# Instance norm on one core: five engine programs without the block around them

## The chip, the cores and the metric

One core of a Trainium2 chip. The metric is the device time of one execution in microseconds (us), as the median of several. The span in a profile is a little shorter, because it runs from the first to the last instruction. Ratios are the mean time of one kernel's runs over the mean of the other's in the same rounds, so not quite the ratio of the medians that are quoted beside them.

## The reference

```python
x: (8, 64, 32, 64, 64) float32          # 512 instances of 131072 values
mean = np.mean(x, axis=(2, 3, 4), keepdims=True)
var  = np.var(x, axis=(2, 3, 4), keepdims=True)
return ((x - mean) / np.sqrt(var + eps)).astype(np.float32)
```

256 MiB come in and 256 MiB go out: 268.44 MB each way.

## The kernel before

A tile is 128 partitions x 8192 values, 4 MiB, with 8 instances of 16 partitions each. Six tiles ("slots") are in flight. SyncE issues the loads. VectorE and ScalarE each sum one half. TensorE averages over partitions. ScalarE squares, takes the root, scales one half and issues the store, while VectorE scales the other half. GpSimd only builds two small matrices at the start. Everything is ordered by hand-placed semaphores (counters that engines count up and wait on), one set per slot. Each engine runs a hardware loop of 10 rounds of six tiles and then five straight-line pieces (three tiles and two half tiles).

The parts that the change touches:

```python
    ctx.enter_context(tc.tile_critical(name="norm"))
    # ... buffers, semaphores, on_vector, on_scalar, on_tensor, over_tiles (cut) ...

    block = ctx.enter_context(nc.Block())

    @block.sync
    def _(eng):
        for s in range(SLOTS):
            eng.dma_start(out=slots[s][:], in_=x_t[s]).then_inc(landed[s], 16)
        # ... loop over the other rounds, each load waiting for its slot's store (cut) ...

    @block.gpsimd
    def _(eng):
        # ... the two matrices and eps, counting up `ready` (cut) ...

    @block.vector
    def _(eng):
        over_tiles(eng, on_vector)

    @block.tensor
    def _(eng):
        eng.wait_ge(ready, READY)
        over_tiles(eng, on_tensor)

    @block.scalar
    def _(eng):
        eng.wait_ge(ready, READY)
        over_tiles(eng, on_scalar, with_target=True)
        for s in range(SLOTS):
            uses = ROUNDS + sum(1 for r in rest if r[3] == s)
            eng.wait_ge(stored[s], 16 * uses)          # all stores have landed
        for s in range(SLOTS, LANES):
            eng.wait_ge(stored[s], 16)
```

An all-engine barrier is a point that no engine passes before all five have come. Three things end this program, one inside the other: the block's exit (line `_compat.py:109` in the profile), the critical section's exit (line 42), and the end of the whole program (the line of the context around the kernel: 271 before, 260 after).

Of the kernel before, what the change touches and what calls it, by code (L numbers as in the profile page):

```python
# [9 lines left out]
def kernel(  # L10
# [6 lines left out]
    nc = tc.nc  # L17
# [11 lines left out]
    SLOTS = 6  # L29
    FULL = P * COLS // n_elem  # L30
    n_tiles = n_inst // FULL
    ROUNDS = (n_tiles - 1) // SLOTS
    LANES = SLOTS + 2
# [10 lines left out]
    def sbuf(name, shape, dtype=fp32):  # L44
        return ctx.enter_context(nc.sbuf_tensor(name, shape, dtype))
# [5 lines left out]
    avg = {n: sbuf(f"avg{n}", [P, P]) for n in (FULL, FULL // 2)}  # L51
# [6 lines left out]
    def semaphores(name, n):  # L58
        return [ctx.enter_context(nc.semaphore(f"{name}{i}")) for i in range(n)]

    ready = semaphores("ready", 1)[0]
# [10 lines left out]
    stored = semaphores("stored", LANES)  # L72
# [61 lines left out]
    def on_tensor(eng, t, lane, n, c1, c2, c16):  # L134
# [17 lines left out]
    rest = [  # L152
        (x_t[k], out_t[k], slots[k % SLOTS][:], k % SLOTS, k // SLOTS + 1, FULL)
        for k in range(ROUNDS * SLOTS, n_tiles - 1)
    ]
# [6 lines left out]
    def over_tiles(eng, step, with_target=False):  # L162
        counts = [
            ctx.enter_context(eng.register(f"{step.__name__}_c{m}")) for m in (1, 2, 16)
        ]
        for c, m in zip(counts, (1, 2, 16)):
            eng.reg_mov(c, m)
        with eng.Fori(0, ROUNDS) as it:
            for s in range(SLOTS):
                more = (out_t[it * SLOTS + s],) if with_target else ()  # L170
                step(eng, slots[s][:], s, FULL, *counts, *more)
            for c, m in zip(counts, (1, 2, 16)):
                eng.reg_add(c, c, m)
        for _, dst, t, lane, c, n in rest:
            more = (dst,) if with_target else ()
            step(eng, t, lane, n, c, 2 * c, 16 * c, *more)

    block = ctx.enter_context(nc.Block())

    @block.sync  # L180
    def _(eng):
        for s in range(SLOTS):
            eng.dma_start(out=slots[s][:], in_=x_t[s]).then_inc(landed[s], 16)
        c16 = ctx.enter_context(eng.register("load_c16"))
        eng.reg_mov(c16, 16)
        with eng.Fori(1, ROUNDS) as it:
            for s in range(SLOTS):
                eng.dma_start(out=slots[s][:], in_=x_t[it * SLOTS + s])._wait_ge(
                    stored[s], c16
                ).then_inc(landed[s], 16)  # L190
            eng.reg_add(c16, c16, 16)
        for src, _, t, lane, c, n in rest:
            behind = lane if lane < SLOTS else last
            uses = c - 1 if lane < SLOTS else ROUNDS
            eng.dma_start(out=t, in_=src)._wait_ge(stored[behind], 16 * uses).then_inc(
                landed[lane], 16
            )

    @block.gpsimd
    def _(eng):  # L200
        count = 0
        for n, m in avg.items():
            split = P // n

            eng.memset(m[:], 1.0 / n_elem).then_inc(ready, 1)  # L205
            count += 1
            for sign in (-1, 1):
                eng.affine_select(  # L208
                    out=m[:],
                    in_=m[:],  # L210
                    pattern=[[sign * split, n], [0, split]],
                    compare_op=Alu.is_ge,
                    fill=0.0,
                    base=0 if sign < 0 else split - 1,
                    channel_multiplier=-sign,
                )._wait_ge(ready, count).then_inc(ready, 1)
                count += 1
        eng.memset(eps_t[:], eps_f).then_inc(ready, 1)

    READY = 3 * len(avg) + 1  # L220

    @block.vector
    def _(eng):
        over_tiles(eng, on_vector)

    @block.tensor
    def _(eng):
        eng.wait_ge(ready, READY)
        over_tiles(eng, on_tensor)

    @block.scalar
    def _(eng):
        eng.wait_ge(ready, READY)
        over_tiles(eng, on_scalar, with_target=True)

        for s in range(SLOTS):
            uses = ROUNDS + sum(1 for r in rest if r[3] == s)
            eng.wait_ge(stored[s], 16 * uses)
        for s in range(SLOTS, LANES):
            eng.wait_ge(stored[s], 16)  # L240


# [33 lines left out]
```

## Time and profile before

| | before |
|---|---|
| time, median of 3 (range) | 1248.47 us (1248.38 to 1248.61) |
| span of the profile | 1246.9 us |
| busiest compute engine | ScalarE, 79% |
| transfers, 120 to 1130 us | share 1.00, 433 GB/s |
| from ScalarE's last wait records to the end | 1245.4 to 1246.9 us |

The lines behind this table stand in the prediction. Read them in this order. First the engine shares: none is full. Then the transfers: they are full. Then the two ends, because a block can only act at its entry and at its exit. A line of an engine's name with q (SPq, ACTq) is a record of that engine's sequencer: a branch, a drain, a semaphore record. The last two numbers ahead of the semicolon are the start of the first and of the last such record. The views round these starts to 0.1 us. Where this text gives hundredths, they are the time stamps that the trace keeps.

### The profile page before, as it was taken

The numbers are of one execution on the slowest core, as the hardware profiler recorded it, in microseconds if no ns is written. First come the engines' busy times: TensorE is split into PE (matmuls) and PEld (weight loads), VectorE is DVE, ScalarE is ACT, GpSimd is POOL, SyncE is SP. The second block draws the span as 40 slices with busy tenths as digits, with TensorE's granted clock in tenths as the row PEclk, the third lists the DMA queues.
The fourth block names the chain that finished last, engine by engine and source line by source line (L and its number), as shares of the span: only waits on it lengthen the run. The fifth ranks groups of instructions, "written<-read, shape, count | busy, mean of one in ns | idle before, by whom it ended". The sixth has DMA issues, their size and how long they took to land.

```text
span 1246.9 us, 1819 instructions
## 1 busy us (share of the span) xinstructions
PE 76.4 (6%) x260; PEld 65.2 (5%) x260; DVE 467.9 (38%) x325; ACT 986.1 (79%) x410; POOL 1.9 (0%) x11
## 2 busy tenths in 40 slices
PE   0000000000000000000000000000000000000000
PEld 0000000000000000000000000000000000000000
DVE  2344334433334334343343433433334333343331
ACT  5888888887787878778777878787787878778774
POOL 0000000000000000000000000000000000000000
DMA  9999999999999999999999999999999999999998
GB/s 403 422 435 427 433 436 435 428 433 436 435 428 433 437 434 429 432 436 435 431 430 436 436 434 425 437 436 435 427 434 436 435 428 433 436 435 428 433 432 376
DMA packets 18723, 536.90 MB, mean 431 GB/s; under 512 B 2081, under 2 KB 2081, under 8 KB 2081
## 3 DMA queue, kind: packets, MB, share of 16 engines
q1 hardware_dynamic: 9360, 268.44, 50.0%
q10 hardware_dynamic: 9360, 268.44, 49.9%
q14 instruction: 3, 0.02, 0.0%
HBM read 268.44 MB, written 268.44 MB: 431 GB/s over the span
## 4 chain that ended last, share of the span: by engine, by line
ACT 48%; DVE 29%; another core or an unknown queue 13%; PE 6%; issue 1%; DMA 1%; ACTq 0%; DVEq 0%; SPq 0%
ACT unused L113 37%; DVE small L79 18%; DVE slot L95 8%; ACT slot L123 4%; ACT unused L107 4%; PE psum L136 3%; PE psum L143 3%; ACT small L120 1%; ACT L120 1%; DMA slot<-in_x_dram 1%; DVE small L89 1%; DVE small L82 1%; DVE small L92 1%; ACTq L130 0%
## 5 line engine op out<-in xcount | busy, mean ns | idle before, releaser
L113 ACT ACTIVATE unused<-slot,small 128x8192 uint8<-128x8192 f32 (+1 forms) x65 | 456.1, 7017 | 90.1 <-DVE small L82 90.1
L79 DVE TENSOR_REDUCE small<-slot 128x1 f32<-128x4096 f32 (+1 forms) x65 | 282.9, 4353 | 164.4 <-DMA slot<-in_x_dram 164.4
L107 ACT ACTIVATE unused<-slot 128x4096 uint8<-128x4096 f32 (+1 forms) x65 | 231.7, 3564 | 82.1 <-DMA slot<-in_x_dram 77.0
L123 ACT ACTIVATE slot<-slot,small 128x4096 f32<-128x4096 f32 (+1 forms) x65 | 243.7, 3749 | 27.6 <-DVE small L92 27.6
L89 DVE RECIPROCAL small<-small 128x1 f32<-128x1 f32 x65 | 10.6, 164 | 533.8 <-ACT small L120 533.8
L95 DVE TENSOR_SCALAR slot<-slot,small 128x4096 f32<-128x4096 f32 (+1 forms) x65 | 154.7, 2379 | 2.4
L136 PE MATMUL psum<-small,avg 128*128 128x2 f32 x130 | 38.2, 363 | 674.1 <-DVE small L79 548.7
L136 PEld LDWEIGHTS psum<-small,avg 128*128 128x128 f32 x130 | 32.6, 311 | 679.6 <-DVE small L79 553.0
L143 PE MATMUL psum<-small,avg 128*128 128x1 f32 x130 | 38.2, 363 | 480.6 <-ACT unused L113 480.6
L143 PEld LDWEIGHTS psum<-small,avg 128*128 128x128 f32 x130 | 32.7, 312 | 486.2 <-ACT unused L113 486.2
L120 ACT ACTIVATE small<-psum,eps_t 128x1 f32<-128x1 f32 x65 | 17.0, 261 | 37.4 <-PE psum L143 37.3
L82 DVE TENSOR_REDUCE small<-psum 128x1 f32<-128x2 f32 x65 | 10.3, 159 | 62.5 <-PE psum L136 62.5
L107 ACT ACT_TABLE_LOAD x10 | 12.8, 1283 | 10.4 <-ACT slot L123 7.1
L120 ACT ACT_TABLE_LOAD x10 | 12.8, 1283 | 0.2
L107 ACT ACTIVATION_READ_ACCUMULATOR unused<-slot 128x1 f32 x65 | 12.1, 186 | 0.0
L113 ACT ACTIVATION_READ_ACCUMULATOR unused<-slot,small 128x1 f32 x65 | 12.1, 186 | 0.0
L92 DVE TENSOR_TENSOR small<-small 128x1 f32<-128x1 f32 x65 | 10.3, 159 | 2.2
L208 POOL TENSOR_SCALAR_AFFINE_SELECT avg<-avg 128x128 f32<-128x128 f32 x4 | 1.3, 324 | 0.3
L205 POOL MEMSET avg<- 128x128 f32 x2 | 0.4, 204 | 0.5 <-SPq L42 0.5
L257 POOL MEMSET const-bfloat16-1.0<- 128x1 bf16 x1 | 0.1, 101 | 0.0
L257 POOL MEMSET const-uint8-127<- 128x1 uint8 x1 | 0.1, 101 | 0.0
L257 POOL MEMSET const-float32-0.0<- 128x1 f32 x1 | 0.1, 98 | 0.3 <-issue 0.3
(2 smaller groups left out, 0.2 us busy)
## 6 DMA issues: line engine op xcount, KB each, us to landing
slot<-in_x_dram SPq DMA_DIRECT2D x63, 4096.0 KB, 52.8
out_dram<-slot ACTq DMA_DIRECT2D x63, 4096.0 KB, 45.3
slot<-in_x_dram SPq DMA_DIRECT2D x2, 2048.0 KB, 55.6
out_dram<-slot ACTq DMA_DIRECT2D x2, 2048.0 KB, 14.7
```

Of the source, the lines that this page charges most:

```text
L79: eng.reduce_sum(out=a[:, 0:1], in_=t[:, :w], axis=mybir.AxisListType.X)._wait_ge(landed[lane], c16).then_inc(summed[lane], 1)
L82: eng.tensor_reduce(out=a[:, 2:3], in_=psum[lane][:, 0:2], axis=mybir.AxisListType.X, op=Alu.add, negate=True,)._wait_ge(meaned[lane], c1) ...
L89: eng.reciprocal(out=a[:, 5:6], in_=a[:, 4:5])._wait_ge(rooted[lane], c1).then_inc(scaled[lane], 1)
L92: eng.tensor_mul(out=a[:, 6:7], in0=a[:, 2:3], in1=a[:, 5:6])._wait_ge(scaled[lane], c1).then_inc(shifted[lane], 1)
L95: eng.tensor_scalar(out=t[:, w:], in0=t[:, w:], scalar1=a[:, 5:6], scalar2=a[:, 6:7], op0=Alu.mult, op1=Alu.add,)._wait_ge(shifted[lane], ...
L107: eng.activation(out=unused[:, w : 2 * w], in_=t[:, w:], func=Act.Identity, accum_out=a[:, 1:2],)._wait_ge(landed[lane], c16).then_inc(sum ...
L113: eng.activation(out=unused[:, : 2 * w], in_=t, func=Act.Square, bias=a[:, 2:3], accum_out=a[:, 3:4],)._wait_ge(centred[lane], c1).then_in ...
L120: eng.activation(out=a[:, 4:5], in_=psum[lane][:, 2:3], func=Act.Sqrt, bias=eps_t[:, 0:1])._wait_ge(varied[lane], c1).then_inc(rooted[lane ...
L123: eng.activation(out=t[:, :w], in_=t[:, :w], func=Act.Identity, scale=a[:, 5:6], bias=a[:, 6:7],)._wait_ge(shifted[lane], c1).then_inc(don ...
L136: eng.matmul(out=psum[lane][:, 0:2], lhsT=avg[n][:], rhs=a[:, 0:2], start=True, stop=True,)._wait_ge(summed[lane], c2).then_inc(meaned[lan ...
L143: eng.matmul(out=psum[lane][:, 2:3], lhsT=avg[n][:], rhs=a[:, 3:4], start=True, stop=True,)._wait_ge(squared[lane], c1).then_inc(varied[la ...
L208: eng.affine_select(out=m[:], in_=m[:], pattern=[[sign * split, n], [0, split]], compare_op=Alu.is_ge, fill=0.0, base=0 if sign < 0 else s ...
```

## The change

Its intent is to shed what a block adds around five engine programs that have their own semaphores anyway. The programs become plain calls, one behind another, inside the critical section.

```diff
-    block = ctx.enter_context(nc.Block())
-
-    @block.sync
-    def _(eng):
+    def load_all(eng):
         ...
-    @block.gpsimd
-    def _(eng):
+    def set_up(eng):
         ...
-    READY = 3 * len(avg) + 1
-    @block.vector
-    def _(eng):
-        over_tiles(eng, on_vector)
-    ... tensor, scalar likewise (cut) ...
+        return count + 1
+
+    load_all(nc.sync)
+    set_by = set_up(nc.gpsimd)
+    over_tiles(nc.vector, on_vector)
+    nc.tensor.wait_ge(ready, set_by)
+    over_tiles(nc.tensor, on_tensor)
+    nc.scalar.wait_ge(ready, set_by)
+    over_tiles(nc.scalar, on_scalar, with_target=True)
+    ... the waits for the stores, on nc.scalar (cut) ...
```

## The prediction

> **What bounds the kernel now.** I read the page from the top, then the transfer queue's waits, a table of stretches, one tile in the timeline, and last the two ends of the program, because the change touches only the ends.
>
> The page first:
>
> ```profile
> span 1246.9 us, 1819 instructions
> PE 76.4 (6%) x260; PEld 65.2 (5%) x260; DVE 467.9 (38%) x325; ACT 986.1 (79%) x410; POOL 1.9 (0%) x11
> ...
> DMA  9999999999999999999999999999999999999998
> ...
> HBM read 268.44 MB, written 268.44 MB: 431 GB/s over the span
> ```
>
> No compute engine is full: ScalarE at 79% comes closest. The transfer engines are at nine tenths or more in 39 of 40 slices. The stretches of the run tell the same with more digits (columns: stretch, its length, busy time of PE, PEld, DVE, ACT, POOL, then clock, transfer share, GB/s):
>
> ```profile
> 1.20:13.50 12.30, 0.00 (x0) 0.00 (x0) 0.00 (x0) 1.28 (x1) 1.51 (x7) 1.00 0.94 384
> ...
> 120.00:1130.00 1010.00, 62.27 (x212) 53.20 (x212) 381.70 (x262) 812.97 (x335) 0.00 (x0) 1.00 1.00 433
> ...
> 1234.00:1246.90 12.90, 0.00 (x0) 0.00 (x0) 0.00 (x0) 0.00 (x0) 0.00 (x0) 1.00 0.70 300
> ```
>
> From 120 to 1130 us the transfer share is 1.00 at 433 GB/s. One tile is 4 MiB in and 4 MiB out, 8.39 MB; 8.39 MB / 433 GB/s = 19.4 us. In the timeline the square pass of two successive late tiles starts at 1160.79 and 1180.21 us, 19.42 us apart, so tiles come at the pace of the transfers. ScalarE has 812.97 / 1010 = 80% in that stretch and sits idle for the rest. The load queue confirms who waits:
>
> ```profile
> SPq L188 <- DMA out_dram<-slot: 1049.1, 54, 52.1
> SPq _compat.py:109 <- PEq _compat.py:109: 84.4, 1, 84.4
> ```
>
> The loads wait 1049.1 us in all for stores to free their slots: slots and bandwidth, not issue speed, set the pace. The second line is the exit of the block, the thing that the change removes: SyncE arrives there after its last load issue and stands 84.4 us. That wait is long and worth nothing, since SyncE has nothing left to do. The chain of waits lists ScalarE at 48% and VectorE at 29%; I give it little weight, because it follows each tile through its compute and cannot name the shared bandwidth ("another core or an unknown queue 13%").
>
> The two ends, by the records of the lines concerned:
>
> ```profile
> L271 SPq COMPARE_BRANCH x1: 37/37/37, 0.9 to 0.9; - x1
> ...
> L183 SPq DMA_DIRECT2D slot<-in_x_dram x6: 389/454/517, 1.0 to 3.5; - x6
> ```
>
> ```profile
> _compat.py:109 POOLq EVENT_SEMAPHORE  x2: 17/17/17, 1245.6 to 1245.7; - x2
> _compat.py:109 POOLq DRAIN  x1: 439/439/439, 2.6 to 2.6; - x1
> _compat.py:109 SPq DRAIN  x1: 125/125/125, 1161.3 to 1161.3; - x1
> ...
> _compat.py:109 ACTq COMPARE_BRANCH  x1: 38/38/38, 1245.4 to 1245.4; - x1
> _compat.py:109 ACTq DRAIN  x1: 8/8/8, 1245.6 to 1245.6; - x1
> _compat.py:109 SPq EVENT_SEMAPHORE  x1: 17/17/17, 1245.8 to 1245.8; - x1
> ```
>
> The number of the line is that of the block's exit. Each engine drains, adds to one semaphore, GpSimd collects and releases them all. Four engines were there long before (GpSimd since 2.6, SyncE since 1161.3); ScalarE, which waits for the last store, comes at 1245.6, and all are out at 1245.8. That is the whole visible cost of the block. Behind it stand the exit of the critical section and two more barriers of the program's end, from 1245.8 to 1246.9, which the change keeps.
>
> **What the Trainium skill says.** "DMA: Bandwidth & Descriptors", section Specifications, gives the fabric ceiling of a core's transfers as 435 GB/s. The trace agrees in that its long stretch stands at 433; that leaves 0.5%, or 6 us of the run, for anything that only improves the flow. "Advanced Engine Details and Errata", section Control Flow Timing, puts an unconditional branch at some 51 ns. The trace does not show any such cost here: the lines of the block's heads (180, 199, 222, 226, 231) have no record at all, and the one branch record before the first load is that of the line above, which carries a semaphore wait and stays. "Runtime: NRT & Kernel Launch", section Instruction fetch mechanics, says that programs stream sequentially and that a taken branch out of the window of two pages stalls for a fetch. The engines' programs lose or keep a handful of instructions each, and the loops keep their bodies, so I expect no new fetch stall; the trace before has 3 packets (0.02 MB) on the instruction queue, and the longest idle stretch of ScalarE at its loop's edge is 0.8 us, where the same step inside the loop takes 0.4 to 0.5.
>
> **The change part by part.** I compared the two built programs engine by engine.
>
> 1. Entry. Before: per engine one jump into its own program; after: none. Loop bodies, their order, semaphores, tiles, the slots and all waits within are the same on every engine. The jumps have no record in the trace (above), so a layout by engine seems to turn them into nothing. The first load is issued at 1.0 us, right behind the branch at 0.9 with 0.1 us between; my estimate of the saving is 0.00, at most 0.05 us.
>
> 2. Middle. Nothing is added or moved. Each engine runs its own queue in the same order as before, although the text now has the five programs one behind another: what follows in the text does not follow in time. Saving 0.
>
> 3. Exit. Removed: the drain and the semaphore record of each engine, and GpSimd's collecting record, eleven records in all. On the path that sets the end lies only: ScalarE's drain (kept in effect, because the critical section's own exit has one), GpSimd's collect and release, SyncE's wake. In the trace's time stamps ScalarE's drain starts at 1245.61, GpSimd's two records at 1245.65 and 1245.73, SyncE wakes at 1245.77 and sets the critical section's exit off at 1245.84; the engines' drains for it follow at 1245.87 to 1245.93, and SyncE has seen them all at 1246.13. After: SyncE will have set that exit off at about 1161, and VectorE, TensorE and GpSimd will have drained for it long before; only ScalarE's drain at 1245.61 is awaited. SyncE then needs one step to see it (0.04 us, as between ScalarE's drain and GpSimd's record above) and one more record (0.07 us, the distance of its records at 1246.06 and 1246.13): 1245.72. So the rest of the end moves from 1246.13 to 1245.72, that is 0.41 us.
>
> Sum: 0.00 + 0 + 0.41 = 0.41 us of 1248.47, or 0.03%. 1248.47 - 0.41 = 1248.06 us.
>
> **The rivals.**
> - The end hides it (gain 0, 1248.5 us): the remaining barriers could wait for something that comes later than ScalarE. For it speaks that two further barriers follow; against it, that four of the five engines arrived at the block's exit long before (at 2.6 to 1231.8 us) and the remaining steps are a serial chain behind ScalarE's drain.
> - The block costs more than its records show (gain 1 to 2 us, about 1247 us): entry jumps with fetches that start the first load late. Against it: the first load stands 0.1 us behind the program's opening barrier, and no record lies in between.
> - The programs' new layout costs a fetch on a loop's back edge (loss). At 9 or 10 edges an engine and some microseconds each it would still fall mostly into idle time, because ScalarE has 20% idle in the long stretch and the loads' issue stands ahead of the data by tens of microseconds. It would have to hit the last tile to be seen; at most 1 us, 1249.5 us.
> - The transfers fall into another rhythm, because something starts some tens of nanoseconds earlier. With the share at 1.00 there is nothing to hide and at most the 6 us above to win; the three runs of before lie within 0.23 us, so the rhythm is stable. Plus or minus 1 us.
> - GpSimd, SyncE, VectorE and TensorE run ahead into the exit of the critical section while others still work. That is safe only if nothing there resets what the others use; the semaphores' reset stands behind a barrier that awaits ScalarE, and I found no race in the built program's check. No effect on the time.
>
> **Range and chances.** The arithmetic gives 1248.06; the spread of runs is 0.23 us, and a different chip or day may move both kernels by about 1 us, which is a choice of mine and not from this trace. So 1248.1, with 1247.0 to 1249.1 for 8 in 10. Two per cent are 25 us: every rival together does not reach it, in either direction. Faster 0.005, same 0.99, slower 0.005.
>
> **What would show each step.** The stretch from 120 to 1130 us must keep share 1.00 and 433 GB/s, and busy times must agree to a few hundredths. The first load must again be issued at 1.0 us. The records of the block's exit line must be gone: 11 fewer instructions, 1808 in all. SyncE's wait of 84.4 us must reappear under the critical section's exit line, of equal length, which shows that the wait was never on the path. ScalarE's last store wait must be followed by the program's end in about 1.1 us where it was 1.5 (1245.4 to 1246.9). The span should come to 1246.5. The prediction is wrong if the last store lands more than 1 us earlier or later, or if new gaps stand at the loops' ends.

## The result, and the profile after

| | before | after |
|---|---|---|
| time, median of 4 (range) | 1248.54 us (1248.38 to 1248.72) | 1247.99 us (1247.95 to 1248.20) |
| ratio | | 0.9996, 95% interval 0.9979 to 1.0013 |
| span | 1246.9 us | 1246.2 us |
| instructions | 1819 | 1808 |

The medians differ by 0.55 us, 0.04%, and the interval alone could not say whether that is real. The trace can, because the records of the exit are placed to hundredths of a microsecond.

The page of the kernel after:

```profile
span 1246.2 us, 1808 instructions
...
HBM read 268.44 MB, written 268.44 MB: 431 GB/s over the span
```

Its stretches, with the columns of the prediction's table of stretches:

```profile
1.20:13.50 12.30, 0.00 (x0) 0.00 (x0) 0.27 (x1) 1.55 (x2) 1.51 (x7) 1.00 0.96 386
...
120.00:1130.00 1010.00, 62.27 (x212) 53.20 (x212) 381.55 (x263) 812.82 (x335) 0.00 (x0) 1.00 1.00 433
```

The middle is as it was: share 1.00, 433 GB/s, ScalarE busy for 812.82 us against 812.97. In the first stretch VectorE and ScalarE have just begun, because the first tile landed a little sooner (at 13.2 us where it was 13.5). That is looked into below.

The head, by the records of the two lines concerned in the kernel after:

```profile
L260 SPq COMPARE_BRANCH  x1: 38/38/38, 0.9 to 0.9; - x1
...
L180 SPq DMA_DIRECT2D slot<-in_x_dram x6: 388/450/498, 1.0 to 3.5; - x6
```

Same branch, same first load. In the time stamps it is issued at 1.03 us in both kernels.

What SyncE's queue waits for in the kernel after (columns: us in total, times, longest):

```profile
SPq L42 <- DVEq L42: 71.8, 1, 71.8
SPq L42 <- ACTq L42: 12.4, 1, 12.4
```

The 84.4 us that SyncE stood at the block's exit are back, 71.8 + 12.4 = 84.2 us, at the exit of the critical section. They were never on the path. SyncE now waits where the program would have it wait next.

The records of the critical section's exit in the kernel after; those of the block's exit are gone:

```profile
L42 SPq EVENT_SEMAPHORE  x3: 17/28/12359, 1161.1 to 1233.1; - x3
L42 SPq NOP  x2: 13/13/13, 0.8 to 1245.5; - x2
L42 POOLq DRAIN  x1: 41/41/41, 1161.1 to 1161.1; - x1
...
L42 ACTq COMPARE_BRANCH  x1: 38/38/38, 1245.2 to 1245.2; - x1
L42 ACTq DRAIN  x1: 8/8/8, 1245.4 to 1245.4; - x1
```

GpSimd, SyncE and the others drain at their own time (GpSimd at 1161.1). One record of SyncE lies open for 12359 ns, until ScalarE's drain at 1245.4, and 0.1 us later SyncE is through (its NOP at 1245.5). The same exit in the kernel before, two lines of it:

```profile
L42 SPq NOP  x2: 13/13/13, 0.8 to 1246.1; - x2
L42 ACTq DRAIN  x1: 8/8/8, 1245.9 to 1245.9; - x1
```

All times of the exit are counted from ScalarE's record that waits for the last store, the second of these two in the kernel before and in the kernel after:

```profile
L240 ACTq EVENT_SEMAPHORE  x2: 38/38/38, 1240.5 to 1245.4; - x2
```

```profile
L229 ACTq EVENT_SEMAPHORE  x2: 38/38/38, 1240.3 to 1245.2; - x2
```

From the trace's time stamps:

| us after that record | before | after |
|---|---|---|
| ScalarE's branch, which carries one more wait | 0.077 | 0.076 |
| ScalarE's first drain | 0.242 | 0.241 |
| SyncE has been released from the block's barrier and signals the next exit | 0.468 | gone |
| ScalarE's drain for the critical section | 0.507 | 0.241 (the same one) |
| SyncE has seen everyone there | 0.762 | 0.320 |
| end of the program | 1.524 | 1.082 |

The block's exit costs 1.524 - 1.082 = 0.442 us. Of this 0.265 us is the barrier itself (0.507 - 0.242). The other 0.177 us is the critical section's exit, which before could begin only behind the barrier (0.762 - 0.507 = 0.255 us, every engine at once) and is now nearly done when ScalarE comes (0.320 - 0.241 = 0.079 us).

### The profile page after: what moved, and what is told of

It reads as the page before. It is cut to its first block, busy times and chain, and to the rows that moved or that the text cites. A ratio compares the mean times of both kernels' runs of the same rounds, so it can differ in the third digit from the quotient of the medians.

```text
span 1246.2 us, 1808 instructions
## 1 busy us (share of the span) xinstructions
PE 76.4 (6%) x260; PEld 65.2 (5%) x260; DVE 468.0 (38%) x325; ACT 986.1 (79%) x410; POOL 1.9 (0%) x11
## 4 chain that ended last, share of the span: by engine, by line
ACT 48%; DVE 29%; another core or an unknown queue 13%; PE 6%; issue 1%; DMA 1%; ACTq 0%; DVEq 0%; SPq 0%
ACT unused L113 37%; DVE small L79 18%; DVE slot L95 8%; ACT slot L123 4%; ACT unused L107 4%; PE psum L136 3%; PE psum L143 3%; ACT small L120 1%; ACT L120 1%; DMA slot<-in_x_dram 1%; DVE small L89 1%; DVE small L82 1%; DVE small L92 1%; ACTq L130 0%
```

## The experiments

Each kernel ran in five rounds beside the kernel before, in three batches on three chips. So runs are compared within a batch. The column "exit" is the time from ScalarE's record that waits for the last store to the end of the program, from that run's trace.

| run | time, median | before, same rounds | difference | exit |
|---|---|---|---|---|
| first comparison (4 runs): before / after | - / 1247.99 | 1248.54 | -0.55 | 1.524 / 1.082 |
| changed again | 1248.15 | 1248.59 | -0.44 | 1.082 |
| one barrier back | 1248.26 | 1248.59 | -0.33 | 1.360 |
| eight barriers at the end | 1250.57 | 1248.59 | +1.98 | 3.678 |
| eight barriers at the head | 1250.76 | 1248.59 | +2.17 | 1.082 |
| before again | 1248.59 | 1248.55 | +0.04 | 1.524 |
| text reversed | 1248.12 | 1248.55 | -0.43 | 1.082 |
| plain drain | 1247.90 | 1248.55 | -0.65 | 0.963 |
| light barrier | 1248.46 | 1248.55 | -0.09 | 1.565 |
| before, third | 1248.57 | 1248.53 | +0.04 | 1.525 |
| changed, third | 1248.13 | 1248.53 | -0.40 | 1.082 |
| block and drain | 1248.47 | 1248.53 | -0.06 | 1.406 |

Theory A: the gain is the barrier at the block's exit and nothing else. Theory B: leaving out the jumps, or the new layout, also makes the transfers start or flow better. B had something to explain: in the first two profiles ScalarE's record for the last store stood 0.2 us earlier after the change, and the first tile had landed 12.20 us after its issue where it took 12.48.

### The changed kernel again

No edit.

> The changed kernel unaltered, run again in five rounds with a fresh profile. Theory A (the gain is the one all-engine barrier at the block's exit, nothing else): from ScalarE's last branch record to the end of the span 1.01 us again, where the kernel before has 1.45; in the time 0.4 to 0.6 us under the kernel before (about 1248.0). In the first comparison another 0.2 us came from an earlier landing of the first tile (12.2 us after issue against 12.5). Theory A calls that scatter: the first landing of this profile may lie anywhere from 13.2 to 13.6 us. Theory B (the layout without jumps also starts the transfers better): first landing again 0.28 us early, at 13.2 us, and time 0.6 us under before.

Measured: 1.082 us of exit again, 1248.15 against 1248.59 us, 0.44 less. The first tile landed at 13.26 us, within what either theory allows. One of the five runs took 1249.97 us; such runs come up again below. The ratio of this run reads 1.0001 because of it, as the mean takes that run in and the median does not. A's sum for the time, 0.44, is met here; the first comparison had 0.11 us more. (The expectation counts from ScalarE's branch, 0.077 us behind the record used here: its 1.01 and 1.45 us are 1.08 and 1.52 here.)

### One barrier back

```diff
     for s in range(SLOTS, LANES):
         nc.scalar.wait_ge(stored[s], 16)
+    nc.all_engine_barrier()
```

> The changed kernel with one all-engine barrier at the end of the critical section, programs still one behind another without a block. Theory A: it is the kernel before again: 1.45 us from ScalarE's last branch record to the end, time within 0.2 us of before (about 1248.5), 1819 instructions. Theory B (layout): it keeps a good part of the gain, first landing at 13.2 us and about 1248.3.

Measured: neither. The exit took 1.360 us, between 1.082 and 1.524, and the time was 0.33 us under before. The instruction count was 1818, one short of the 1819 that Theory A expected. The trace names the missing one. In the kernels before and after, ScalarE's waits for the stores sit on four semaphore records and, one of them, on the branch to the exit. (It is the wait for the first slot, whose last store had landed at 1212.5 us in the kernel before, so it holds nothing up.) That branch starts 0.077 us behind the record before it, and the drain follows it only 0.165 us later. In this kernel the barrier follows the waits directly: there is no branch, that wait shares a record with another, and the drain comes 0.077 us behind that record:

```profile
L231 ACTq DRAIN  x1: 8/8/8, 1245.2 to 1245.2; - x1
```

So one barrier back costs 1.360 - 1.082 + 0.165 = 0.443 us, against 0.442 for the block's barrier, and the branch that was lost pays 0.165 us of it. A barrier alone is the block's whole cost, but this edit also took away a cost that nobody had listed.

### Eight barriers at the end

```diff
+    for _ in range(8):
+        nc.all_engine_barrier()
```

> The changed kernel with eight all-engine barriers at the end of the critical section. Theory A: each costs 0.44 us in series behind ScalarE's wait for the last store, so 8 x 0.44 = 3.5 us over the changed kernel: about 1251.5, and 4.5 us from ScalarE's last branch record to the end. Rival (barriers behind the last store overlap with something of the launch or with the store's end, as the remaining ones may): under 1 us in the time, about 1248.5.

Measured: 1250.57 us, 1.98 us over before and 2.42 over the changed kernel in the same rounds, where 3.5 were expected. The rival (under 1 us) falls: nothing at the end hides a barrier. But the size is off. The records of the barriers' line, and the exit behind them:

```profile
L232 ACTq DRAIN  x8: 8/8/8, 1245.4 to 1247.6; - x8
...
L232 ACTq EVENT_SEMAPHORE  x8: 17/17/17, 1245.5 to 1247.9; - x8
...
L42 ACTq DRAIN  x1: 8/8/8, 1247.9 to 1247.9; - x1
```

ScalarE drains for the first barrier at 1245.4 us and for the critical section at 1247.9, eight barriers later (1245.358 and 1247.946 in the time stamps): 2.588 us, so 0.32 us each. Against the kernel with one barrier, seven more add 3.678 - 1.360 = 2.318 us, or 0.331 each. My 0.44 was the barrier together with the exit of the critical section that must start over behind it, and that part is paid once and not eight times.

### Eight barriers at the head

```diff
+    for _ in range(8):
+        nc.all_engine_barrier()
     load_all(nc.sync)
```

> The changed kernel with eight all-engine barriers ahead of the first load. Theory A, extended to the head: the first load is issued 8 x 0.44 = 3.5 us later, at 4.5 us, and as the transfers are the bound all the way nothing makes it up: 1251.5. Rival: the compute engines have 20% idle time and the slots run dry anyway, so that the middle takes some of it back: 1248.5 to 1250.

The barriers and the first load in this kernel:

```profile
L218 SPq DRAIN  x8: 7/7/7, 1.0 to 3.3; - x8
...
L180 SPq DMA_DIRECT2D slot<-in_x_dram x6: 388/434/522, 3.7 to 6.1; - x6
```

The first load leaves at 3.65 us in place of 1.03, which is 2.62 us later, or 0.33 for each barrier (again not 0.44). The time is 1250.76 us, 2.61 over the changed kernel of the same rounds (1248.15). So the whole delay reaches the end. The idle fifth of ScalarE gives nothing back, because the stretch from 120 to 1130 us is bound by the transfers and not by ScalarE. A cost at the entry would have been paid in full. The change had none to take away there.

### The kernel before again

No edit.

> The kernel before, unaltered, as a kernel of its own, to show what two equal programs differ by. So far its one profile has the first tile's landing 12.48 us after the issue, and five kernels without the block have 12.18 to 12.36. Theory A (scatter): this profile lies inside or near 12.2 to 12.5, and the time within 0.2 us of the other runs of before. Theory B (the layout helps the first transfer): 12.5 again. Either: 1.52 us from ScalarE's record for the last store to the end.

Measured: 1248.59 us, 0.04 from the other runs of before; exit 1.524 us; first tile 12.36 us behind its issue, no longer 12.48. Two equal programs differ by 0.04 us in the median here and in the third round of runs. That is what a difference of medians must be held against.

### The text reversed

```diff
-    load_all(nc.sync)
-    set_by = set_up(nc.gpsimd)
-    over_tiles(nc.vector, on_vector)
-    ... tensor, then scalar and its waits (cut) ...
+    set_by = 3 * len(avg) + 1
+    ... scalar and its waits, then tensor (cut) ...
+    over_tiles(nc.vector, on_vector)
+    set_up(nc.gpsimd)
+    load_all(nc.sync)
```

> The changed kernel with the five programs written in the reverse order (ScalarE first, SyncE last), the same instructions on each engine. Theory A: nothing changes, 1.08 us from ScalarE's record for the last store to the end, first load issued at 1.03 us, time as the changed kernel (about 1248.1). Theory B (place in the text matters, through jumps or instruction fetch): the first load leaves later than 1.03 us, by 0.05 us or more, or new gaps at the loops' ends.

Measured: exit 1.082 us, first load at 1.03 us, 1248.12 us, 0.43 under before. What stands first in the text does not matter. Each engine takes its own part, and SyncE, now written last, starts as early as ever.

### A plain drain on ScalarE

```diff
     for s in range(SLOTS, LANES):
         nc.scalar.wait_ge(stored[s], 16)
+    nc.scalar.drain()
```

> The changed kernel with one drain of ScalarE behind its waits for the stores. In the runs so far the last of these waits sits on a branch, which then takes 0.165 us from its start to the next record where the others take 0.077; the run with one barrier back had no such branch and so kept 0.16 us of the gain. Theory A2 (a branch that carries a wait costs on the path): with the drain the waits pair up on records, the branch is gone, and from ScalarE's record for the last store to the end it takes 1.00 us (0.08 less than the changed kernel's 1.08; 0.16 would fall to 0.92 if the drain itself were free). Time 1247.9 to 1248.1. Rival: the added drain costs what the branch did: 1.08.

The drain of the added line in this kernel, and the critical section's exit:

```profile
L230 ACTq DRAIN  x1: 8/8/8, 1245.3 to 1245.3; - x1
...
L42 ACTq DRAIN  x1: 8/8/8, 1245.3 to 1245.3; - x1
```

There is no branch record any more. The added drain carries the wait that was on the branch, and the exit's own drain follows 0.047 us behind it (both at 1245.3). The exit takes 0.963 us, 0.119 less than the changed kernel, between the two figures expected; the rival (1.08) falls. The time is 1247.90 us, 0.65 under before and 0.22 under the reversed text of the same rounds, of which the exit explains 0.12. This is the best of all kernels run, by a margin of no practical weight. That the branch costs time was thus found in one run and confirmed in another. That the wait makes it slow, as the expectation says, is not shown, and the trace speaks against it: the wait was met 33 us before, and in the kernel before eight of SyncE's nine loop branches (line 186), which carry no wait, take the same 0.164 to 0.165 us from their start to the next record (the ninth leaves the loop for a load that waits).

### The block's lighter barrier

```diff
-    block = ctx.enter_context(nc.Block())
+    block = ctx.enter_context(nc.Block(no_gpsimd_drain=True))
```

> The kernel before with the block's own option for a barrier of semaphores alone, without GpSimd's drain. Theory A: GpSimd's drain stood at 2.6 us, more than 1240 us off the path, so dropping it saves nothing; the cost is the serial collect and release: 1.4 to 1.6 us from ScalarE's record for the last store to the end, time within 0.2 us of before. Rival: the drain in the barrier is what costs: near the changed kernel's 1.08 us and 1248.1. The first landing gives one more sample of a kernel with the block: Theory B wants 12.5, scatter anything from 12.2.

Measured: exit 1.565 us, 0.04 longer than before, and a time 0.09 under before. GpSimd's drain was off the path, as said, and a separate semaphore record on each engine takes its place. The option saves nothing here. The first tile landed 12.13 us after its issue, earlier than in any kernel without the block. Theory B, which tied an early landing to the missing block, falls on this number; the two kernels without the block in the same batch took 12.29 and 12.33 us.

### Before and changed, once more

No edits.

> The kernel before once more. In the profiles so far ScalarE's record for the last store stands at 1245.34 to 1245.45 us in three kernels with the block and at 1245.14 to 1245.28 in six without (those with barriers at the head left out or shifted back), which is no part of the exit. Scatter: with this profile the two ranges meet, that is, it stands below 1245.3 here or above 1245.3 in the next. A real effect of the block on the flow: 1245.35 to 1245.5 again. Time within 0.2 us of before.

> The changed kernel once more, for the same question. Scatter: ScalarE's record for the last store anywhere from 1245.1 to 1245.5 us. A real effect: 1245.1 to 1245.3 again. From there to the end 1.08 us; time 0.4 to 0.5 us under before.

Both profiles fell on one of the rare slower executions (1249.94 and 1250.19 us), so the question was not answered as put. ScalarE's record for the last store stood at 1246.71 and 1247.38 us. The exits were untouched, 1.525 and 1.082 us, and the medians fit: 1248.57 and 1248.13. The first tile landed 12.47 us after issue in the changed kernel here, as late as in the first profile of before. So for the landing it is scatter.

The stretches of such an execution at the end say where the time goes; first the kernel before in its first profile, then this slower one:

```profile
1241.00:1243.00 2.00, 0.00 (x0) 0.00 (x0) 0.00 (x0) 0.00 (x0) 0.00 (x0) 1.00 0.92 393
1243.00:1245.00 2.00, 0.00 (x0) 0.00 (x0) 0.00 (x0) 0.00 (x0) 0.00 (x0) 1.00 0.10 41
1245.00:1246.20 1.20, 0.00 (x0) 0.00 (x0) 0.00 (x0) 0.00 (x0) 0.00 (x0) 1.00 0.00 0
```

```profile
1241.00:1243.00 2.00, 0.00 (x0) 0.00 (x0) 0.00 (x0) 0.00 (x0) 0.00 (x0) 1.00 0.92 393
1243.00:1245.00 2.00, 0.00 (x0) 0.00 (x0) 0.00 (x0) 0.00 (x0) 0.00 (x0) 1.00 0.06 25
1245.00:1246.20 1.20, 0.00 (x0) 0.00 (x0) 0.00 (x0) 0.00 (x0) 0.00 (x0) 1.00 0.06 27
```

The last three numbers of a line are the clock, the transfer share and GB/s. A share of 0.06 is one of 16 transfer engines (1 / 16 = 0.0625). The bulk is done by 1243 us in both; then, on average, one or two engines work off what is left, until 1244.9 us in the one and 1246.2 in the other (ends of the last packets, from the trace). The end only shows this delay; it grows over the whole run. Each store counts its semaphore up 16 times. For the first slot's stores the sixteenth count comes 0.14 us later in the slower run than in the first profile of before in the third round, 1.20 in the sixth and 2.44 in the tenth, while the fifteenth stays within 0.16 us in all ten. So the last of the 16 parts of a store, and it alone, lags more and more. Why it does so in some executions of either kernel stays open.

### Block and drain

```diff
         for s in range(SLOTS, LANES):
             eng.wait_ge(stored[s], 16)
+        eng.drain()
```

> The kernel before, with its block, and one drain of ScalarE behind its waits for the stores, which took 0.12 us off the changed kernel by removing the branch that carries a wait. If that saving and the barrier are independent parts, it takes 0.12 us off here too: 1.40 us from ScalarE's record for the last store to the end, where before has 1.52, and a time of about 1248.45. If the saving needs the missing barrier: 1.52.

Measured: exit 1.406 us, 0.118 less than before's 1.524, so the two savings add up independently. The time came 0.06 us under before where 0.12 were due, which is within the spread. ScalarE's record for the last store stood at 1245.24 us, with the block in place, among those of the kernels without it in ordinary executions (1245.14 to 1245.28). With that, the 0.2 us by which the stores seemed to end earlier is scatter too, as far as one profile per kernel can say. The times agree: with 0.44 us at the exit and another 0.2 ahead of it, the repeated comparisons would have shown some 0.64 us and not 0.40 to 0.44.

## Why the prediction was right

The measured 1247.99 us lies 0.07 us from the predicted 1248.06, well inside the range of 1247.0 to 1249.1. That the number is so close is partly luck: the four runs of the kernel after spread over 0.25 us. The steps are what counts:

1. Entry, 0.00 us: right. The first load is issued at 1.03 us in both, and the reversed text leaves it there. The eight barriers at the head show that a real cost there would have counted in full.
2. Middle, 0: right. Share 1.00, 433 GB/s, ScalarE's busy time the same to 0.15 us in 813. The sign asked for agreement to a few hundredths, which was tighter than the scatter: two profiles of the kernel before (812.97 and 812.85 us) differ by 0.12 themselves. No new gap stands at the loops' ends: ScalarE's idle time ahead of its table loads there is 7.1 us in both pages. The 6 us that the prediction leaves for a better flow are an estimate from the 435 GB/s of the Trainium skill ("DMA: Bandwidth & Descriptors", Specifications); no run tests that ceiling.
3. Exit, 0.41 us: the mechanism was right, and the term a little small; the traces have 0.442. The part that was mis-sized is the last step. I allowed 0.11 us from ScalarE's drain to SyncE's last record there, in two steps. It took 0.079, since SyncE's record was already lying open when ScalarE came.
4. The signs named in advance: 1808 instructions, yes; SyncE's wait back under the other line, yes, in two pieces that sum to 84.2 in place of 84.4; about 1.1 us from the last store's wait to the end, yes, 1.08. The span came to 1246.2 and not 1246.5 (unrounded 1246.24 and 1246.48). The trace puts 0.21 of these 0.24 us ahead of the exit, and that is the scatter above; the rest is the mis-sized step.

The rivals: "the end hides it" fell on the eight barriers at the end and on the trace; "the block costs more than its records show" fell on one barrier back, where a barrier without a block cost 0.443; the layout and the rhythm fell on the reversed text and on the repeated runs. The prediction's sentence that the line of the block's exit is the "whole visible cost of the block" fits only half: 0.265 of the 0.442 us are those records, and the rest is the next exit, which the barrier had kept from starting. Its arithmetic had this, its sentence did not. What it overlooked is ScalarE's branch to the exit, which the change keeps and which is worth 0.12 us.

How sure is 0.44 us in the time? Leave aside the executions that took over 1249 us; they occur in both programs. Then every run of the changed program (in its three submissions and in reversed text) took between 1247.95 and 1248.30 us, and every run of the program before took at least 1248.33. The four differences of medians are 0.55, 0.44, 0.43 and 0.40.

## What to carry to other kernels

Ask of a structural change which instructions it removes from each engine's own stream and where the last engine to arrive stands; a wait of 84 us at a barrier can be worth nothing, and the barrier behind the last arrival costs its serial hops, here 0.33 us each. In this kernel, bound by its transfers, eight barriers counted in full at either end (2.42 us at the end and 2.61 at the head); no run put one in the middle. When an experiment that puts a cost back returns only part of it, compare the records one by one before doubting the theory: here it had removed a second cost by accident.

## What the Trainium skill lacked or had wrong

- "Runtime: NRT & Kernel Launch" (the preamble/postamble breakdown) times the launch's own barriers alone. Of these it gives some 355 ns for the pass through five engines, which is near what was measured here. No page that I found has the cost of an all-engine barrier inside a kernel: 0.33 us each in series (eight at the head moved the first load by 2.62 us), and 0.442 us for one at a block's exit, with the exit behind it.
- "Advanced Engine Details and Errata", Control Flow Timing, gives about 51 ns for an unconditional branch and about 108 ns for a compare-and-branch, and does not say from where to where. Here the jumps between program parts have no record and no cost (first load at 1.03 us with and without them). The record of ScalarE's compare-and-branch is 38 ns long and takes 0.165 us from its start to the next record; putting a drain in its place saved 0.12 us in two kernels, which is near the page's 108 ns.
- "DMA: Bandwidth & Descriptors", Where 436 GB/s comes from, says that the HBM side (some 358 GB/s) binds for transfers between HBM and the core's memory. One core alone moved 433 GB/s here, in and out together, so that limit did not bind. The same page's section Measured has 425 GB/s for a single core; the two passages do not fit together without the words "with both cores streaming".
- The same page, Latency and other measured facts, calls two of the 16 transfer engines usually slower and guesses at the software-driven path as the cause. Here all data went over hardware queues, and still the sixteenth count of the last store came 0.97 us after the fifteenth in the first profile of before; after 1243 us one or two engines on average (share 0.06 to 0.10) still worked for some 2 us, and for 3 to 4 us in the executions that took 1.4 to 2 us longer. The trace does not name the engine, and no page that I found says how much this costs at a kernel's end.
